# Loading w_down in pairs of whole rows, and accumulating both halves of its columns at once

## The chip, the cores and the metric

The kernel runs on one core of a Trainium2 chip. What is measured is device time in microseconds (us). A core has a tensor engine (PE; its weight loads are shown as PEld), a vector engine (DVE), a scalar engine (ACT), GpSimd (POOL) and the SP engine, which in this kernel issues nearly all the DMA transfers. Transfers run on 16 DMA engines that all queues share. SBUF has 128 partitions; matmuls accumulate in PSUM, in banks of 128 x 512 float32.

## The reference

One decoder block for 256 tokens of width 1024, in float32. A mixer (attention and a convolution), a cross-attention into a memory, and then a mixture of 32 experts, which is the part that matters here:

```python
def expert_step(y, args):
    wg, wu, wd, ge = args
    out = (jax.nn.silu(t @ wg) * (t @ wu)) @ wd
    return y + ge[:, None] * out, None

y, _ = lax.scan(expert_step, jnp.zeros_like(t), (w_gate, w_up, w_down, gates))
```

`w_gate` and `w_up` are [32, 1024, 512] and `w_down` is [32, 512, 1024]: 2 MiB for each matrix of each expert, 192 MiB in all. Each token goes to 2 of the 32 experts; the kernel reads the weights of all 32. The block ends with a residual and an RMS norm.

## The kernel before, in words

**Weights.** Every weight goes through `Ring`: a list of loads in a fixed order (`ring.queue`), 25 slots of SBUF (8 KB in each partition, 1 MiB in all) and `pump`, which issues the next load on SP's queue (line 121) as soon as a slot is free. `ring.take` hands a loaded slot to the code that uses it, and `ring.done` frees it, which issues the next load of the list. So the order of the loads is written out by hand, and SP issues them in that order. In the trace every weight tile is called `w`.

**The experts.** They run in eight groups (`for g in range(NGR)`, line 1140) of four. A group's 24 loads are queued in the order of use: eight of `w_gate` (key `eg`), eight of `w_up` (`eu`), eight of `w_down` (`ed`), 1 MiB each. `w_gate` and `w_up` load in halves of the contraction: partition p gets 4 of its 8 rows, which lie one behind the other in memory (4 x 512 x 4 bytes). `w_down` loads in halves of the columns (`down_cols`): partition p gets 512 of the 1024 columns of 4 rows, so 4 pieces of 2 KB that lie 4 KB apart.

**The products.** The four experts of a group stand side by side on the tensor engine, each in 32 of its 128 columns (32 token places for each expert, `tile_position=(0, 32 * q)`). A float32 matmul shows as two records in the trace. Line 1151 computes `eg` and `eu`, each in one PSUM bank. `hidden_T` takes silu of the one times the other and transposes it to `hT` (lines 985 to 992). Line 1181 computes `ed` = hidden times `w_down`, one column half after the other, each 16 matmuls in a bank of its own; `combine` (lines 1000 and 1002) copies that bank to SBUF on ACT (`yd`) and adds it to the tokens' sums `Y`, which stay in PSUM over all groups. Then `start_group` picks and gathers the tokens of the next group (`tgp`, line 968), transposes the gates (`GSp`, line 975), and the next group begins.

**What sets the order.** A scheduler places each engine's instructions by the order of the code; four PSUM banks are shared by `eg`, `eu`, `hTp`, `ed`, `tgp` and `GSp` in turn, and the tiles `tg` and `yd` share one buffer, so a group's gather waits for the `Y` products of the group before.

**The last group** (g = 7) loads `w_down` in four column slices (512, 256, 128, 128), expert by expert in its matmuls, and the residual and the norm follow slice by slice. Before the last slices it also loads `final_g`, on ACT's queue (line 1163).

Of the kernel before, what the change touches and what calls it, by code (L numbers as in the profile page):

```python
# [18 lines left out]
PSUM = bass.MemoryType.PSUM  # L19

P = 128
# [37 lines left out]
class Ring:  # L59
    """Weight loads in a fixed order through slots of SBUF: a load starts as soon as a slot is free.  # L60
    Larger tensors of the first phase live in slots too, so that their memory joins as they end."""
# [13 lines left out]
    def grow(self, stack, name, n, floats=SLOT):  # L75
        """n more slots, on memory that earlier pools have left"""
        for i in range(n):
            pool = stack.enter_context(self.tc.tile_pool(name="%s_%d" % (name, i), bufs=1, reuse_waits="tile"))
            self.size[pool] = floats
            self.free.append(pool)  # L80
        self.pump(self.first)

    def hold(self, n):
        """keep the next n slots that are freed for spare()"""
        self.held += n

    def spare(self, shape, dt=F32):
        """a slot for another tensor [P, *shape]: the tensor and the slot"""
        pool = self.kept.popleft() if self.kept else self.free.popleft()
        return self.view(pool, shape, dt), pool  # L90
# [7 lines left out]
    def queue(self, key, shape, src, within=None):  # L98
        """within: the load of an earlier key whose slot this one shares, and the columns there"""
        self.todo.append((key, shape, src, within))  # L100

    def pump(self, limit=1000):
        while self.todo and limit:
            key, shape, src, within = self.todo[0]
            if within is None:
                pool = next((p for p in self.free if self.size[p] >= math.prod(shape)), None)
                if pool is None:
                    return
                self.free.remove(pool)
                v = self.view(pool, shape, F32)  # L110
                self.live.append((key, v, pool))
                v = v[:, :, :src.shape[2]]
            else:
                v = next(e[1] for e in self.live if e[0] == within[0])[:, :, within[1]]
            limit -= 1
            self.todo.popleft()
            # the very first in two parts, so that the arithmetic starts sooner
            n = 1 if self.begun else 2
            self.begun = True
            for k in range(0, shape[0], shape[0] // n):  # L120
                self.nc.sync.dma_start(v[:, k:k + shape[0] // n], src[:, k:k + shape[0] // n])
# [18 lines left out]
class Pair:  # L140
    """An operand [P, NJ, S] of 24 significant bits as two of 12; each half of its rows in one slot."""
# [16 lines left out]
def down_cols(g):  # L158
    """column slices of w_down's loads; finer at the end"""
    return [(0, 512), (512, 512)] if g < NE // 4 - 1 else [(0, 512), (512, 256), (768, 128), (896, 128)]  # L160


def body(tc, a, out):
# [55 lines left out]
    # U[s, t] = 1 where s <= t  # L219
# [3 lines left out]
    # the same in bf16, which holds 0 and 1 exactly  # L223
# [4 lines left out]
    # the tensor engine's clock rests when it idles: products nobody reads keep it up meanwhile  # L228
# [16 lines left out]
    # router columns: NG group columns, padding that never wins, NE expert columns  # L245
# [4 lines left out]
    # group of each expert column  # L250
# [18 lines left out]
    # the chunks of v and the forget gate are wider than the others  # L269
# [30 lines left out]
    for g in range(NE // 4):  # L300
        for kind, w in (("eg", w_gate), ("eu", w_up)):
            for h in range(2):
                for q in range(4):
                    wv = w[4 * g + q].rearrange("(p j) f -> p j f", j=NJ)
                    ring.queue((kind, g, h, q), (4, DE), wv[:, 4 * h:4 * h + 4, :])
        for n, (c0, w) in enumerate(down_cols(g)):
            for q in range(4):
                wv = w_down[4 * g + q].rearrange("(p j) n -> p j n", j=4)
                if n < 3:
                    ring.queue(("ed", g, n, q), (4, 256 if n == 2 else w), wv[:, :, c0:c0 + w])  # L310
                else:
                    ring.queue(None, (4, w), wv[:, :, c0:c0 + w], (("ed", g, 2, q), slice(128, 256)))
# [30 lines left out]
    def rsqrt(src, scale, shape, name, pool=None, out=None):  # L343
        """(src * scale + eps) ** -0.5, with one Newton step on the vector engine"""
        pool = pool or small
        r = pool.tile(shape, F32, tag=name + "r", name=name + "r")
        A.activation(r, src, AF.Ln, scale=scale, bias=eps_t)
        A.activation(r, r, AF.Exp, scale=-0.5)
        v = pool.tile(shape, F32, tag=name + "v", name=name + "v")
        V.tensor_scalar(v, src, scale, EPS, op0=OP.mult, op1=OP.add)  # L350
        t = pool.tile(shape, F32, tag=name + "t", name=name + "t")
        if shape[1] == 1:
            V.scalar_tensor_tensor(t, r, r, v, op0=OP.mult, op1=OP.mult)
        else:
            V.tensor_mul(t, r, r)
            V.tensor_mul(t, t, v)
        V.tensor_scalar(t, t, -0.5, 1.5, op0=OP.mult, op1=OP.add)
        out = r if out is None else out
        V.tensor_mul(out, r, t)
        return out  # L360

    def ssq(ss, src, eng):
        """ss [P, 1] = sum of squares along src [P, n]"""
# [8 lines left out]
    def ssq_rstd(src, n, name):  # L372
        """src [P, NT, n] -> rstd [P, NT]"""
# [11 lines left out]
    def split(v):  # L385
        """hi + lo == v exactly, each of 12 significant bits; a few rows of v at a time"""
# [17 lines left out]
    def put_split(pair, j, src, g):  # L404
        """split (src * g) into pair[:, j]"""
# [3 lines left out]
    def transposed(pair, src, g, k0, k1, cols, name):  # L409
        """pair[:, k] = split of g[:, k] * (cols(k) of src)^T, for k in k0 .. k1"""  # L410
# [14 lines left out]
    def normed(src, dst):  # L425
        """rmsnorm, without the gain, of src [P, NT, D] into dst"""
# [11 lines left out]
    def wstat(key, pair, name):  # L438
        """256 columns of a projection, transposed: two [P, S] in PSUM"""
# [10 lines left out]
    def astat(key, pair, n, name, outs=None, first=True, last=True, j0=0, bank=mm_ps):  # L450
        """n columns of a projection, natural: NT tiles [P, n] in PSUM"""
# [85 lines left out]
    # log_sigmoid(f) = min(f, 0) - ln(1 + exp(-|f|)) and its cumulative sum  # L537
# [14 lines left out]
    def cum_2():  # L552
        """-c by head"""
# [6 lines left out]
    def cum_3():  # L560
        """-c the same in every partition: [masked block 0 | block 0 | masked block 1]"""
# [266 lines left out]
    def x_blocks(i, k0, k1):  # L828
        """tT[:, k] = gain * (columns of block k)^T for the tokens of tile i"""
# [24 lines left out]
    # the last products tile by tile, so that the first tile's steps run beside the second's  # L854
# [42 lines left out]
    # experts outside the token's group drop out  # L897
# [15 lines left out]
    # place of each token in its expert's list, from 1  # L913
# [20 lines left out]
    # the experts' sum, [NT][2] tiles [P, 512], grows in PSUM over all groups  # L934
    Yp = [[psY.tile([P, 512], F32, name="Y%d%d" % (i, n)) for n in range(2)] for i in range(NT)]

# [1 line left out]
    last_pick = [None]  # L938

    def pick_mats(key_v, n, eng, SR=None):  # L940
        """S picks tokens into slots; SR has 1/rms for its ones"""
# [11 lines left out]
    def gate_mats(Sv, g_v, n):  # L953
        """the gates in place of S's ones"""
# [7 lines left out]
    def gather(SR, n, tg, j0=0, j1=NJ, step=4):  # L962
        """the normed tokens that SR picks, transposed: tg [P, NJ, n]"""
# [17 lines left out]
    def hidden_T(pg, pu, n, sg=None, hTt=None):  # L981
        """silu(pg) * pu, transposed with f = 4 p + j: [P, 4, n]"""
# [15 lines left out]
    def combine(pd, n, GST, yd, outs, w, first=False, last=False):  # L998
        """add the slots' gated outputs to their tokens in outs, [P, w] for each token tile"""
# [18 lines left out]
    def overflow_table():  # L1018
        """blocks of CAP tokens beyond the first of each expert: their number, experts and thresholds"""
# [29 lines left out]
    def overflow(ntot, eidx, thr):  # L1049
        """the general path: one block of one fuller expert after another"""  # L1050
# [41 lines left out]
    fin = {}  # L1092

    def out_slice(n, c0, w, outs, base, last):
        """Z = outs + base in some columns, and the sum of its squares; all but the last times the gain"""
# [18 lines left out]
    # the group's probability and the two experts' shares of it  # L1114
# [25 lines left out]
    for g in range(NGR):  # L1140
# [29 lines left out]
        for n, (c0, w) in enumerate(down_cols(g)):  # L1170
# [5 lines left out]
            # tile by tile side by side, or as the last weights come in  # L1176
# [16 lines left out]
            else:  # L1193
                for i in range(NT):
                    V.tensor_add(X[:, i, c0:c0 + w], Ycols(c0, w)[i], X[:, i, c0:c0 + w])
                if end:
                    # mean of squares + eps, but for the last columns
# [48 lines left out]
```

## Time and profile before

| what | value |
|---|---|
| device time, 3 runs | 706.91, 707.68, 707.87 us; median 707.68 |
| span of the profiled execution | 705.3 us |
| what lies around the span, to the median | 2.4 us |
| PE busy in the span | 583.4 us (83%) |
| DMA, mean over the span | 337 GB/s, 237.36 MB |
| group 2, from its first `eg` matmul to that of group 3 | 333.26 to 394.79 |
| last group, first `eg` matmul to the end of the span | 642.53 to 705.3 |

The profiled execution's own time is its span, 705.3 us, and the 2.4 us around it that the median of the runs has more. Times below count from the start of the span. A row of the timeline joins neighbouring instructions of one kind: start, length, engine, line, operation, output and inputs, count, and in brackets how long the engine sat idle before it and what ended that. A row of the windows view gives, for one stretch, the busy time and count of each engine, then the granted clock of the tensor engine as a share of full speed, the share of the 16 DMA engines that was busy, and GB/s. The first part of the kernel (mixer, cross-attention, routing) ends at about 250 us; the expert groups fill the rest.

### The profile page before, as it was taken

The page shows a single profiled execution, that of the slowest core. Times are in us where ns is not written, and L with a number is a line of the kernel's source. Part 1 is how long each engine was busy: PE and PEld are TensorE (multiplying, and loading weights), DVE is VectorE, ACT ScalarE, POOL GpSimd, SP SyncE. Part 2 cuts the span into 40 slices and gives each one's busy share as a digit, 9 for nine tenths or more (in the row PEclk, how much of TensorE's full clock was granted, in tenths as well). Part 3 has the DMA queues.
Part 4 walks back from the last instruction along what each step waited for, and adds up shares of the span by engine and source line. Part 5 has one row for each costly group of instructions (what it writes and reads, how often), then busy time and mean ns, then how long its engine had stood idle before and what let it go on. Part 6 is the DMA issues. An engine that isn't in the chain of part 4 may idle for free. (4 is left out here: it accounts for less than half of the span.)

```text
span 705.3 us, 8963 instructions
## 1 busy us (share of the span) xinstructions
PE 583.4 (83%) x3517; PEld 344.8 (49%) x3517; DVE 224.2 (32%) x496; ACT 175.0 (25%) x384; POOL 122.1 (17%) x106
## 2 busy tenths in 40 slices
PE   7999999899899999998657856866796787679685
PEld 4999889678897752525112511511251151125124
DVE  5799789785765620401000100100010010001013
ACT  6474765484444600010000000000000000000023
POOL 5556435493434100000000000000000000000000
PEclk9999999999999999999999999998998999999898
DMA  7979630666756979999999999999999999999993
GB/s 255 358 186 367 235 112 11 228 239 234 302 172 263 339 305 419 409 390 420 418 393 407 419 409 390 421 419 392 408 417 410 390 420 419 392 407 417 413 341 117
DMA packets 91164, 237.36 MB, mean 337 GB/s; under 512 B 11996, under 2 KB 36720, under 8 KB 74736
## 3 DMA queue, kind: packets, MB, share of 16 engines
q1 hardware_dynamic: 90688, 235.72, 87.6%
q10 hardware_dynamic: 432, 1.05, 0.4%
q8 instruction: 28, 0.46, 0.3%
q14 instruction: 16, 0.13, 0.1%
HBM read 235.70 MB, written 1.05 MB: 336 GB/s over the span
## 5 line engine op out<-in xcount | busy, mean ns | idle before, releaser
L1151 PE MATMUL eu<-w,tg 128*32 128x512 f32 x512 | 100.2, 680 | 47.8 <-DMA w<-in_w_up 47.8
L396 POOL TENSOR_TENSOR WL<-w,WH 128x512 fp32r<-128x512 f32 (+1 forms) x80 | 112.2, 1414 | 112.4 <-ACT WH L394 93.0
L1181 PE MATMUL ed<-w,hT 128*32 128x512 f32 (+2 forms) x576 | 90.8, 549 | 29.3 <-DMA w<-in_w_down 23.8
L394 ACT CAST WH<-w 128x512 fp32r<-128x512 f32 (+1 forms) x120 | 72.8, 619 | 47.7 <-PE pmk L401 7.3
L1151 PEld LDWEIGHTS eu<-w,tg 128*32 128x32 f32 x512 | 21.3, 122 | 122.9 <-DMA w<-in_w_up 83.1
L950 POOL TENSOR_SCALAR SR<-S,r 128x128 f32<-128x128 f32 x7 | 4.2, 603 | 397.9 <-PE Y L1002 397.9
L1181 PEld LDWEIGHTS ed<-w,hT 128*32 128x32 f32 x576 | 25.6, 109 | 88.1 <-DMA w<-in_w_down 41.3
L986 DVE TENSOR_TENSOR sgm<-sgm,eu 128x512 f32<-128x512 f32 x8 | 5.5, 688 | 196.4 <-PE eu L1151 167.3
L968 PEld LDWEIGHTS tgp<-SR,X 128*128 128x128 f32 x256 | 61.8, 335 | 11.6 <-ACT SR L949 10.7
L968 PE MATMUL tgp<-SR,X 128*128 128x128 f32 x256 | 63.5, 410 | 4.4 <-ACT SR L949 4.4
L1151 PE MATMUL eg<-w,tg 128*32 128x512 f32 x512 | 63.0, 595 | 3.2 <-DMA w<-in_w_gate 3.2
L492 DVE SCALAR_TENSOR_TENSOR cacc<-z,pT,cacc 128x256 f32<-128x256 f32 x116 | 56.4, 486 | 2.6
L956 DVE TENSOR_TENSOR S<-S,GT 128x256 f32<-128x256 f32 x8 | 3.4, 425 | 133.9 <-POOL SR L950 133.8
L396 DVE TENSOR_TENSOR WL<-w,WH 128x512 fp32r<-128x512 f32 (+1 forms) x40 | 37.5, 938 | 15.6 <-ACT WH L394 15.5
L992 ACT COPY hT<-hTp 128x512 f32<-128x512 f32 x8 | 4.7, 585 | 149.2 <-PE hTp L989 149.2
L1000 ACT COPY yd<-ed 128x512 f32<-128x512 f32 (+2 forms) x18 | 9.7, 538 | 124.0 <-PE ed L1181 124.0
L1002 PE MATMUL Y<-yd,GST 128*128 128x512 f32 (+1 forms) x64 | 30.9, 605 | 8.5 <-ACT yd L1000 8.5
L985 ACT ACTIVATE sgm<-eg 128x512 f32<-128x512 f32 x8 | 4.8, 597 | 131.9 <-PE eg L1151 131.9
L1151 PEld LDWEIGHTS eg<-w,tg 128*32 128x32 f32 x512 | 16.3, 109 | 41.3 <-issue 32.3
L969 DVE TENSOR_TENSOR tg<-tgp,g_norm_ffn_g 128x512 f32<-128x512 f32 (+1 forms) x18 | 11.4, 633 | 53.0 <-PE tgp L968 53.0
L1002 PEld LDWEIGHTS Y<-yd,GST 128*128 128x128 f32 x64 | 10.8, 189 | 28.8 <-ACT yd L1000 21.5
L400 PE MATMUL pmk<-w,WH 128*128 128x256 f32 x64 | 18.8, 294 | 0.0
(332 smaller groups left out, 949.3 us busy)
## 6 DMA issues: line engine op xcount, KB each, us to landing
w<-in_w_up SPq DMA_DIRECT2D x64, 1024.0 KB, 19.9
w<-in_w_gate SPq DMA_DIRECT2D x64, 1024.0 KB, 14.3
w<-in_w_down SPq DMA_DIRECT2D x60, 1024.0 KB, 14.4
w<-in_w_mkv SPq DMA_DIRECT2D x8, 1024.0 KB, 13.3
w<-in_w_in SPq DMA_DIRECT2D x7, 1024.0 KB, 10.4
w<-in_w_out SPq DMA_DIRECT2D x4, 1024.0 KB, 10.8
w<-in_w_mq SPq DMA_DIRECT2D x4, 1024.0 KB, 13.2
w<-in_w_mo SPq DMA_DIRECT2D x4, 1024.0 KB, 6.1
```

What stands on the lines that cost most here:

```text
L394: A.copy(hi, src)
L396: (V if nsplit[0] % 3 == 0 else G).tensor_tensor(lo, src, hi.bitcast(F32), op=OP.subtract)
L400: T.matmul(o, L[0], R[0], start=first, stop=False)
L492: V.scalar_tensor_tensor(dst, z[:, cb, t:t + S], pT[:, 4 * t + cb:4 * t + cb + 1], acc, op0=OP.mult, op1=OP.add)
L968: T.matmul(t[:, j], X[:, i, ja + j::NJ], SR[:, i], start=i == 0, stop=i == NT - 1)
L969: V.tensor_tensor(tg[:, ja:ja + step], t, gff[:, ja:ja + step].unsqueeze(2).to_broadcast([P, step, n]), op=OP.mult)
L985: A.activation(sg, pg[0:n], AF.Silu)
L986: V.tensor_mul(sg, sg, pu[0:n])
L1000: ins = A.copy(yd[:, :w], pd[0:n, :w])
L1002: T.matmul(outs[i], GST[:, i], yd[:, :w], start=first, stop=last)
L1151: T.matmul(o[32 * q:32 * q + 32], tg[:, j, 32 * q:32 * q + 32], ws[q][0][:, jj], start=j == 0, stop=j == NJ - 1, tile_position=(0, 32 * q))
L1181: T.matmul(o[32 * q:32 * q + 32, :w], hh[:, j, 32 * q:32 * q + 32], ws[q][0][:, j, :w], start=j == 0, stop=j == 3, tile_position=(0, 32 * q))
```

## The change

In groups 0 to 6, `w_down` loads in halves of its rows instead of its columns: partition p gets 2 of its 4 rows with all 1024 columns, 8 KB in one piece. There are still eight loads of 1 MiB for each group, through the same slots. The matmuls take the two rows of a load (`jj`) one after the other, and for each row both column halves `n`, in two PSUM banks that are open at once; the first half of the loads is freed after 16 matmuls, the second after the other 16, and both `combine` steps come after all 32. The last group's loads and products stay as they are. The diff also drops comments and docstrings, which are left out here.

```diff
+        if g < NE // 4 - 1:
+
+            for h in range(2):
+                for q in range(4):
+                    wv = w_down[4 * g + q].rearrange("(p j) n -> p j n", j=4)
+                    ring.queue(("ed", g, h, q), (2, D), wv[:, 2 * h:2 * h + 2, :])
+            continue
         for n, (c0, w) in enumerate(down_cols(g)):
             for q in range(4):
                 wv = w_down[4 * g + q].rearrange("(p j) n -> p j n", j=4)
...
         yd = new_yd(P)
-        for n, (c0, w) in enumerate(down_cols(g)):
+        if not last:
+            os_ = [e_ps("ed") for _ in range(2)]
+            for h in range(2):
+                ws = [ring.take(("ed", g, h, q)) for q in range(4)]
+                for jj in range(2):
+                    j = 2 * h + jj
+                    for n in range(2):
+                        for q in range(4):
+                            T.matmul(os_[n][32 * q:32 * q + 32], hh[:, j, 32 * q:32 * q + 32],
+                                     ws[q][0][:, jj, 512 * n:512 * n + 512],
+                                     start=j == 0, stop=j == 3, tile_position=(0, 32 * q))
+                for q in range(4):
+                    ring.done(ws[q][1])
+            for n in range(2):
+                combine(os_[n], P, GST, yd[:, n], Ycols(512 * n, 512), 512, g == 0, False)
+        for n, (c0, w) in enumerate(down_cols(g) if last else []):
             o = e_ps("ed")
```

On SP's queue the loads stay in their places. Around the `w_down` loads of group 0 the queue reads so (128 partitions x 4 pieces of 512 before, x 2048 in one now):

```order
 L121 DMA w<-in_w_gate 128x2048 x7
 L121 DMA w<-in_w_up 128x2048 x7
-L121 DMA w<-in_w_down 128x4x512 x8
+L121 DMA w<-in_w_down 128x2048 x8
 L121 DMA w<-in_w_gate 128x2048 x8
```

Only the shape of the `w_down` loads moved; it is now that of `w_gate` and `w_up`. The same exchange stands in each of the seven groups.

On the tensor engine, group 2 before, from the hidden layer's transpose to the next group's first product (`hTp` the transpose, `ed` the products with `w_down`, `Y_309x` the four sums, `tgp` the gather, `GSp` the gates):

```order
L989 MATMUL hTp<-ident,sgm 128x128 x4
L1181 MATMUL ed<-w,hT 32x512 x17
L1002 MATMUL Y_3090<-yd,GST 128x512
L1002 MATMUL Y_3092<-yd,GST 128x512
L1181 MATMUL ed<-w,hT 32x512 x15
L1002 MATMUL Y_3091<-yd,GST 128x512
L1002 MATMUL Y_3093<-yd,GST 128x512
L968 MATMUL tgp<-SR,X 128x128 x16
L975 MATMUL GSp<-ident,S 128x128 x2
L1151 MATMUL eg<-w,tg 32x512 x32
```

And the same place after the change, where line 1181 has become 1185, 1002 has become 1009 and the others moved by 7:

```order
L996 MATMUL hTp<-ident,sgm 128x128 x4
L1185 MATMUL ed<-w,hT 32x512 x32
L1009 MATMUL Y_3090<-yd,GST 128x512
L1009 MATMUL Y_3092<-yd,GST 128x512
L1009 MATMUL Y_3091<-yd,GST 128x512
L1009 MATMUL Y_3093<-yd,GST 128x512
L975 MATMUL tgp<-SR,X 128x128 x16
L982 MATMUL GSp<-ident,S 128x128 x2
L1158 MATMUL eg<-w,tg 32x512 x32
```

The first pair of `Y` products moved from the middle of the `ed` matmuls to behind all of them; the number of matmuls is the same.

## Rows read from the trace of the kernel before

**Rows 1.** The page's slices: 40 equal parts of the span, 17.6 us each.
```profile
PE   7999999899899999998657856866796787679685
PEclk9999999999999999999999999998998999999898
DMA  7979630666756979999999999999999999999993
```

**Rows 2.** The page's DMA counts and issues: loads, KB of each, us to landing.
```profile
DMA packets 91164, 237.36 MB, mean 337 GB/s; under 512 B 11996, under 2 KB 36720, under 8 KB 74736
w<-in_w_up SPq DMA_DIRECT2D x64, 1024.0 KB, 19.9
w<-in_w_gate SPq DMA_DIRECT2D x64, 1024.0 KB, 14.3
w<-in_w_down SPq DMA_DIRECT2D x60, 1024.0 KB, 14.4
```

**Rows 3.** The windows view: while w_up, w_down, w_gate/w_up and again w_down land.
```profile
402.00:418.00 16.00, 8.96 (x48) 1.83 (x40) 0.00 (x0) 0.60 (x1) 0.00 (x0) 1.00 1.01 419
422.00:441.00 19.00, 12.08 (x56) 3.01 (x48) 0.69 (x1) 1.17 (x2) 0.00 (x0) 1.00 1.05 392
444.00:461.00 17.00, 15.58 (x82) 9.85 (x77) 2.47 (x5) 0.99 (x2) 0.60 (x1) 1.00 1.02 421
606.00:625.00 19.00, 14.43 (x71) 3.94 (x72) 0.69 (x1) 1.17 (x2) 0.00 (x0) 0.91 1.05 388
```

**Rows 4.** The tensor engine's timeline, group 3 and the start of group 4.
```profile
419.79 3.62 PE L1151 MATMUL eu<-w,tg 128*32 128x512 f32 x26 [1.47 <-DMA w<-in_w_up]
...
434.99 1.98 PE L1002 MATMUL Y<-yd,GST 128*128 128x512 f32 x4 [0.53 <-ACT yd L1000]
441.44 3.62 PE L1181 MATMUL ed<-w,hT 128*32 128x512 f32 x26 [1.63 <-DMA w<-in_w_down]
...
456.34 4.49 PE L1151 MATMUL eg<-w,tg 128*32 128x512 f32 x38
461.38 3.19 PE L1151 MATMUL eg<-w,tg 128*32 128x512 f32 x25 [0.56 <-DMA w<-in_w_gate]
...
466.37 1.05 PE L1151 MATMUL eu<-w,tg 128*32 128x512 f32 x2 [1.36 <-DMA w<-in_w_up]
468.87 1.04 PE L1151 MATMUL eu<-w,tg 128*32 128x512 f32 x2 [1.45 <-DMA w<-in_w_up]
```

**Rows 5.** The windows view: PE's work in one whole group, 3.
```profile
394.79:456.34 61.55, 43.88 (x240) 16.88 (x239) 3.16 (x7) 2.75 (x5) 0.60 (x1) 1.00 1.02 408
```

**Rows 6.** The windows view around the start of the groups.
```profile
250.00:260.00 10.00, 10.00 (x64) 6.61 (x67) 1.50 (x4) 0.00 (x0) 0.00 (x0) 1.00 0.59 219
260.00:270.00 10.00, 10.00 (x94) 2.93 (x86) 0.08 (x1) 0.60 (x1) 0.00 (x0) 1.00 1.02 425
```

**Rows 7.** The view of `in_w_down`, stretch 220 to 252: issues, ns, first and last start.
```profile
L121 SPq DMA_DIRECT2D w<-in_w_down x8: 539/540/622, 224.4 to 243.5; - x8
```

**Rows 8.** SP's waits from 250 to 262: us in total, times, longest.
```profile
SPq L121 <- PE eg L1151: 10.5, 1, 10.5
```

**Rows 9.** SP's timeline: load issues of groups 3 and 4.
```profile
402.34 27.20 SPq L121 DMA_DIRECT2D w<-in_w_down  x8
...
443.95 17.79 SPq L121 DMA_DIRECT2D w<-in_w_up  x8
```

**Rows 10.** The tensor engine's timeline: w_down products of groups 0 and 1.
```profile
272.09 4.48 PE L1181 MATMUL ed<-w,hT 128*32 128x512 f32 x34 [0.67 <-ACT hT L992]
...
318.35 3.62 PE L1181 MATMUL ed<-w,hT 128*32 128x512 f32 x26 [0.94 <-DMA w<-in_w_down]
```

**Rows 11.** The tensor engine's timeline: group 7, last w_up load to first w_down products.
```profile
668.81 3.62 PE L1151 MATMUL eu<-w,tg 128*32 128x512 f32 x26 [1.47 <-DMA w<-in_w_up]
673.27 0.75 PE L989 MATMUL hTp<-ident,sgm 128*128 128x128 f32 x4 [0.84 <-DVE sgm L986]
```

**Rows 12.** The chain that ended last, its first piece: start, us, what.
```profile
674.80 8.91 PE ed L1181 x34
```

## What the change will do to the time: the prediction

> **What bounds the kernel now.** I read the page's slices first, then the windows view stretch by stretch, then the tensor engine's timeline with what ended its idle times. In the slices the DMA engines are at 9 tenths from the sixteenth slice on, that is from 15 x 17.6 = 264 us, nearly to the end, while PE mostly stands at 6 to 8 [rows 1]. So the expert groups are fed by a stream of weights. The timeline confirms it: in a steady group PE waits for `w_up`, then for `w_down`, a little for `w_gate`, and again for `w_up` [rows 4], and of the 61.55 us from one group's first `eg` product to the next it is busy 43.88 [rows 5].
>
> The stream is not equally fast everywhere. Where `w_up` or `w_gate` lands it moves 419 and 421 GB/s, where `w_down` lands 392 and 388 [rows 3]. The busy share of the engines does not fall there (1.05 against 1.01 and 1.02): they work as much and move less. The page says what differs: its packets under 8 KB are 74,736 of 91,164 [rows 2], and the 16,428 others are nearly the 128 loads of `w_gate` and `w_up` with 128 packets of 8 KB each (16,384). A `w_down` load of 1 MiB in pieces of 2 KB is 512 packets.
>
> The time of a load comes cleanest from the ends of PE's waits. The last `w_up` load of group 3 lets PE go at 419.79, the last of its eight `w_down` loads at 441.44, the last of the next eight, `w_gate`, at 461.38 [rows 4]. Eight loads with pieces of 2 KB thus took 21.65 us, eight with pieces of 8 KB 19.94.
>
> **The change, part by part.**
>
> *Eight loads with pieces of 8 KB.* A new `w_down` load has just the shape of a `w_gate` load, on both sides: in memory 8 KB in one piece for each partition, 16 KB from one partition to the next; in SBUF one slot. I give it the same time: 21.65 - 19.94 = 1.71 us saved in each group whose `w_down` loads lie in the saturated stream. The windows give less, since their stretches are not cut exactly at the loads: 8.39 MB at 390 GB/s (the mean of the two rows) are 21.51 us, at 420 GB/s 19.97, a saving of 1.54. I take 1.71, as it has all eight loads in it, and keep 1.54 for the range.
>
> The row on packet size can be set against a rule. The Trainium skill (page "DMA: Bandwidth & Descriptors", section "Why small descriptors are slow") puts a fixed overhead of about three cycles on each packet, beside one cycle for 32 bytes: as an estimate 67 cycles for 2 KB and 4 x 64 + 3 = 259 for 8 KB, so 3.4% less time, 0.73 us in a group and 703.3 us for the kernel. The two waits above show 7.9%; by them it is the sum that follows. The rows decide, and the rule's result is among the rivals.
>
> *How many groups.* Seven groups change, but group 0 lies elsewhere. Its loads are issued from 224.4 to 243.5 [rows 7], and its `w_down` products begin at 272.09 after a wait for `hT`, not for a load [rows 10]. Between 250 and 260 the stream stands at 219 GB/s and a busy share of 0.59 [rows 6], because SP waits 10.5 us for slots that PE's first `eg` products free [rows 8]; from 260 on it is saturated at 425 [rows 6]. Landing group 0's `w_down` earlier moves nothing: 0 us. Groups 1 to 6 are in the stream; the last `w_down` load of group 1 already ends a wait of PE [rows 10]. So 6 x 1.71 = 10.3 us.
>
> *The Y products, moved.* Before, the first pair (1.98 us, after 0.53 us for ACT) lay between the two halves of the loads, in time that PE would have waited [rows 4]. Now both pairs come behind the last load. PE's way from there to the next group's first `eg` product was 456.34 - 441.44 = 14.90 us; it grows by 1.98, to 16.9 (the second ACT copy runs beside the first pair, so one such wait stays, as before). The first half of `eg` then ends not at +19.4 but at +21.4, some 1.4 us after the last `w_gate` load at +19.94: the 0.56 us of waiting at 461.38 goes, and the next `w_up` waits, 1.36 and 1.45 us for single loads, take up what is left [rows 4]. The stream itself doesn't wait for PE there. Cost 0. Without that cover it would be 6 x 1.4 = 8.4 us.
>
> *Two banks at once.* The number of matmuls and weight loads stays, four experts still stand side by side, and the banks used in a group are as many. I cost it at nothing: 34 records of line 1181 take 4.48 us [rows 10], and 34 are the 32 of the first half and two of the second, so PE passes from one bank to the other without a stall. A gain is excluded, as nothing is left out. The upper end is each record alone, half of the 1.05 us that two take one after the other [rows 4]; that is the last rival. I take the row of line 1181 itself.
>
> *SP's queue.* Eight `w_down` issues occupy it for 27.20 us, eight `w_up` for 17.79 [rows 9]. The new ones should go as the latter. SP runs ahead of the transfers (19.9 and 14.4 us from issue to landing [rows 2]), so nothing waits for that: 0. It will ask for slots some 5 us earlier; these were freed a whole group before, since 25 slots hold 24 loads of a group and one more.
>
> *The end.* The last group is as before. From its last `w_up` load, which ends a wait at 668.81, PE runs without a wait for a load through `hT` [rows 11] and the `w_down` products that begin the final chain [rows 12]. So 705.3 - 668.81 = 36.5 us behind the last `w_up` load stay, and what the stream gains before it reaches the end whole.
>
> Sum: the profiled execution has a span of 705.3 us; 705.3 - 10.3 = 695.0. With the 2.4 us that the median of the runs has beyond that span, 697.4 us. By the lower saving 6 x 1.54 = 9.2, 698.5.
>
> **The rivals.**
>
> *Part of the difference stays.* If only half of the 1.71 us is due to the packets, and the rest to where `w_down` lies or how it shares the engines, 5.1 us go: 702.6. For it: the trace has no `w_down` load in large pieces. Against: the new loads equal those of `w_gate` in everything that the trace shows. The skill's three cycles, above, would end near here.
>
> *No change.* The loads keep 388 to 392 GB/s because it is the tensor and not the piece that is slow: 707.7. The Trainium skill speaks for this one (same page, "Specifications"): it puts the smallest transfer for line rate at 512 bytes, and 2 KB is well above. By that rule the two rates in the windows should be one; the trace disagrees, with 390 against 420 GB/s.
>
> *Group 0 counts too*, if its loads hold up the `w_gate` loads behind them: 7 x 1.71 = 12.0, 695.7. Against: SP waits for slots there [rows 8].
>
> *Slower: PE becomes the bound.* If a matmul could not run beside its neighbour of another bank, the 64 records of a group's `ed` would take 64 x 0.525 = 33.6 us in place of some 8.1 (4.48 and 3.62 [rows 10]). PE's 43.88 [rows 5] would be 69.4, more than the stream's new 61.55 - 1.71 = 59.8; over six groups 6 x (69.4 - 61.55) = 47 us, about 755. It decides once `ed` costs more than 8.1 + 17.7 = 25.8 us in a group, since PE has 61.55 - 43.88 = 17.7 us free; below that the stream hides it. Against: PE passes from bank to bank now without a stall.
>
> A smaller matter lies in all cases: the granted clock is at its lower level (1.2 of 2.4 GHz) in short stretches, as in group 6, where the mean over 19 us is 0.91 [rows 3]. In front of a load it costs nothing, as PE waits there anyway; in the last 36.5 us it would cost a microsecond or two.
>
> **How the numbers follow.** My forecast gets 0.84, half of the difference 0.06, no change 0.04, group 0 as well 0.03, slower 0.03. The forecast's own range is 696.3 to 698.9: the lower saving, the runs' spread of about 0.5 us to either side, and a microsecond earlier should the deeper queue help. For 8 in 10 I give 695.5 to 700.5, which takes in group 0 and a slow stretch at the end, and leaves out half, no change and slower, 0.13, and a rest. About 0.2%, or 1.4 us, is what a measurement here can tell from no change: faster 0.93 (0.84 + 0.06 + 0.03), the same 0.04, slower 0.03.
>
> **What would show it.** In the new profile the windows where `w_down` lands should read near 420 GB/s in groups 1 to 6, as for `w_gate`, and only the last group's below; packets under 8 KB should fall by 7 x 8 x 512 = 28,672. From the last `w_up` load's wait to the last `w_down` load's should be 19.9 us, from group to group about 59.8, and the way from the last `w_down` load to the next `eg` product 16.9. SP should issue eight `w_down` loads in about 18 us. Group 0's times should stay, as should the 36.5 us at the end. The prediction is wrong if `w_down` stays at 390 GB/s, if PE's waits for loads vanish from the groups (then PE bounds), or if the stream shows gaps that end with a slot.

## The result, and the profile after

| | before | after |
|---|---|---|
| device time, median of 4 runs | 707.71 us (706.91 to 707.87) | 697.25 us (696.63 to 698.14) |
| ratio, with its 95% interval | | 0.9837 [0.9801, 0.9873] |
| span of the profiled execution | 705.3 us | 695.1 us |
| last `w_up` load of the last group ends PE's wait | 668.81 | 658.67 |
| PE busy in the span | 583.4 us | 598.3 us |
| DMA, mean over the span | 337 GB/s | 341 GB/s |

The kernel is faster by 10.5 us; 697.4 was predicted, and a span of 695.0. PE is busy for 15 us longer and the kernel still ends sooner, so the time did not come from PE. One run of the experiment `g0old`, at 1701.43 us, and one of the kernel before, at 986.55 us, lie far outside all others and are left out below. I read the page first, for the packets and the issues, and its slices for the stream.

The page of the kernel after: the slices of 17.4 us (DMA busy share, GB/s), and its count of packets.

```profile
DMA  7979640765747879999999999999999999999993
GB/s 253 358 185 365 229 144 1 241 225 206 304 168 257 339 287 420 421 419 418 420 421 418 420 421 421 418 421 420 422 418 420 419 421 419 419 420 419 405 344 114
DMA packets 69660, 237.36 MB, mean 341 GB/s; under 512 B 11996, under 2 KB 36720, under 8 KB 46064
```

Packets under 8 KB fell from 74,736 [rows 2] to 46,064, by the 28,672 that the changed loads were to lose. From the sixteenth slice on the stream moves 418 to 422 GB/s up to the last group; the DMA engines' busy share reads 9 as before [rows 1]. Now two stretches in which `w_down` lands, the start of the groups and one whole group. The columns are those of [rows 3]: the last three are granted clock, DMA share and GB/s.

```profile
402.00:418.00 16.00, 8.85 (x52) 1.97 (x54) 0.00 (x0) 0.00 (x0) 0.00 (x0) 1.00 1.01 418
594.00:612.00 18.00, 13.32 (x68) 3.51 (x68) 0.69 (x1) 0.59 (x1) 0.00 (x0) 1.00 1.01 419
250.00:260.00 10.00, 10.00 (x64) 6.63 (x67) 1.51 (x4) 0.00 (x0) 0.00 (x0) 1.00 0.55 211
392.44:452.32 59.88, 47.13 (x240) 18.68 (x239) 3.16 (x7) 2.76 (x5) 0.60 (x1) 1.00 1.01 420
```

While `w_down` lands the stream now moves 418 and 419 GB/s at a share of 1.01, where it moved 392 and 388 at 1.05 [rows 3]. The slow start, 211 GB/s at 0.55, is still there [rows 6]. The last row is group 3 from its first `eg` product to the next group's: 59.88 us in place of 61.55, with 47.13 us of PE in it in place of 43.88 [rows 5].

The tensor engine's timeline over group 3 after, from the last `w_up` load to the next group's first `w_up` loads (1158 was 1151, 1185 was 1181, 1009 was 1002).

```profile
416.45 3.62 PE L1158 MATMUL eu<-w,tg 128*32 128x512 f32 x26 [1.45 <-DMA w<-in_w_up]
...
422.35 3.48 PE L1185 MATMUL ed<-w,hT 128*32 128x512 f32 x12 [0.68 <-ACT hT L999]
426.42 4.40 PE L1185 MATMUL ed<-w,hT 128*32 128x512 f32 x24 [0.60 <-DMA w<-in_w_down]
431.41 1.90 PE L1185 MATMUL ed<-w,hT 128*32 128x512 f32 x4 [0.59 <-DMA w<-in_w_down]
...
436.40 3.62 PE L1185 MATMUL ed<-w,hT 128*32 128x512 f32 x20 [0.59 <-DMA w<-in_w_down]
439.95 3.70 PE L1009 MATMUL Y<-yd,GST 128*128 128x512 f32 x8
444.22 7.94 PE L975 MATMUL tgp<-SR,X 128*128 128x128 f32 x32 [0.57 <-ACT SR L956]
...
452.32 7.22 PE L1158 MATMUL eg<-w,tg 128*32 128x512 f32 x63
...
461.33 1.05 PE L1158 MATMUL eu<-w,tg 128*32 128x512 f32 x2 [1.10 <-DMA w<-in_w_up]
463.83 1.05 PE L1158 MATMUL eu<-w,tg 128*32 128x512 f32 x2 [1.45 <-DMA w<-in_w_up]
```

Three readings. From the last `w_up` load to the last `w_down` load: 436.40 - 416.45 = 19.95 us, where [rows 4] had 21.65. From there to the next `eg` product: 452.32 - 436.40 = 15.92 us, where it was 14.90. And the wait of `eg` for `w_gate` (0.56 us at 461.38 [rows 4]) is gone; the next `w_up` loads end waits of 1.10 and 1.45 us, so PE has caught up with the stream.

SP's timeline after: eight issues of `w_down`.

```profile
399.02 17.77 SPq L121 DMA_DIRECT2D w<-in_w_down  x8
```

The eight `w_down` issues stand in a stretch of 17.77 us in place of 27.20 [rows 9]; those of `w_gate` and `w_up` behind them in 17.79 us each. Such a stretch also holds what SP waits between two issues. On the page, the time from issue to landing is now this, the same for `w_gate` and `w_up`:

```profile
w<-in_w_down SPq DMA_DIRECT2D x60, 1024.0 KB, 19.9
```

The tensor engine's timeline after, groups 0 and 1, and then the last group from its last `w_up` load: the `ed` products of its four column slices.

```profile
272.11 7.07 PE L1185 MATMUL ed<-w,hT 128*32 128x512 f32 x64 [0.68 <-ACT hT L999]
...
316.44 3.62 PE L1185 MATMUL ed<-w,hT 128*32 128x512 f32 x20 [0.59 <-DMA w<-in_w_down]
...
658.67 3.62 PE L1158 MATMUL eu<-w,tg 128*32 128x512 f32 x26 [1.49 <-DMA w<-in_w_up]
...
664.65 8.83 PE L1203 MATMUL ed<-w,hT 128*32 128x512 f32 x36 [0.78 <-ACTq L1060]
...
676.13 3.75 PE L1203 MATMUL ed<-w,hT 128*32 128x256 f32 x36
...
681.36 1.99 PE L1203 MATMUL ed<-w,hT 128*32 128x128 f32 x24
...
684.36 2.46 PE L1203 MATMUL ed<-w,hT 128*32 128x128 f32 x32
```

Group 0 begins its `ed` products at 272.11, as at 272.09 before [rows 10]; group 1's last `w_down` load comes 318.35 - 316.44 = 1.91 us earlier; the last `w_up` load of the last group 668.81 - 658.67 = 10.14 us earlier [rows 11]. Behind that the end takes 695.1 - 658.67 = 36.4 us, as before (36.5). The gain grows group by group: the last `w_up` loads of groups 2 to 7 let PE go 1.62, 3.34, 5.62, 7.12, 8.49 and 10.14 us earlier than before, in steps of 1.37 to 2.28 us. It is made in the stream, in the six groups named, and nowhere else.

### The profile page after: what moved, and what is told of

It reads as the page before. It is cut to its first block, busy times and chain, and to the rows that moved or that the text cites. A ratio compares the mean times of both kernels' runs of the same rounds, so it can differ in the third digit from the quotient of the medians.

```text
span 695.1 us, 8957 instructions
## 1 busy us (share of the span) xinstructions
PE 598.3 (86%) x3517; PEld 353.8 (51%) x3517; DVE 224.1 (32%) x496; ACT 175.1 (25%) x384; POOL 122.2 (18%) x106
## 2 busy tenths in 40 slices
DMA packets 69660, 237.36 MB, mean 341 GB/s; under 512 B 11996, under 2 KB 36720, under 8 KB 46064
## 3 DMA queue, kind: packets, MB, share of 16 engines
q10 hardware_dynamic: 432, 1.05, 0.4%
HBM read 235.70 MB, written 1.05 MB: 341 GB/s over the span
## 5 line engine op out<-in xcount | busy, mean ns | idle before, releaser
L1158 PE MATMUL eu<-w,tg 128*32 128x512 f32 x512 | 102.7, 715 | 45.0 <-DMA w<-in_w_up 45.0
L1185 PE MATMUL ed<-w,hT 128*32 128x512 f32 x448 | 89.1, 598 | 16.9 <-DMA w<-in_w_down 12.2
L975 PEld LDWEIGHTS tgp<-SR,X 128*128 128x128 f32 x256 | 62.0, 336 | 10.8 <-ACT SR L956 10.0
L1185 PEld LDWEIGHTS ed<-w,hT 128*32 128x32 f32 x448 | 22.0, 109 | 79.0 <-issue 39.3
L1158 PE MATMUL eg<-w,tg 128*32 128x512 f32 x512 | 61.0, 594 | 0.0
L1158 PEld LDWEIGHTS eg<-w,tg 128*32 128x32 f32 x512 | 18.4, 109 | 34.0 <-issue 27.4
L1009 PE MATMUL Y<-yd,GST 128*128 128x512 f32 (+1 forms) x64 | 29.0, 593 | 1.1 <-ACT yd L1007 1.1
L1009 PEld LDWEIGHTS Y<-yd,GST 128*128 128x128 f32 x64 | 11.4, 189 | 18.8 <-issue 10.5
## 6 DMA issues: line engine op xcount, KB each, us to landing
w<-in_w_up SPq DMA_DIRECT2D x64, 1024.0 KB, 19.9
w<-in_w_gate SPq DMA_DIRECT2D x64, 1024.0 KB, 19.9
w<-in_w_down SPq DMA_DIRECT2D x60, 1024.0 KB, 19.9
```

The source lines that it names most:

```text
L975: T.matmul(t[:, j], X[:, i, ja + j::NJ], SR[:, i], start=i == 0, stop=i == NT - 1)
L1009: T.matmul(outs[i], GST[:, i], yd[:, :w], start=first, stop=last)
L1158: T.matmul(o[32 * q:32 * q + 32], tg[:, j, 32 * q:32 * q + 32], ws[q][0][:, jj], start=j == 0, stop=j == NJ - 1, tile_position=(0, 32 * q))
L1185: T.matmul(os_[n][32 * q:32 * q + 32], hh[:, j, 32 * q:32 * q + 32], ws[q][0][:, jj, 512 * n:512 * n + 512], start=j == 0, stop=j == 3, ti ...
```

## The experiments

Each kernel below is the one after with one edit, timed in five rounds against the kernel before on the same chip. The theory: each packet of a load has a fixed price on the DMA engines, and 8 KB pieces have a quarter of the packets of 2 KB pieces. The rivals: that the gain came with the new order of the products or of the rows; that it belongs to the tensor `w_down` and not to the pieces; that the gaps in memory cost and not the packets; that group 0 or SP's queue had a part in it. SP's queue has no run of its own; the traces have to settle it.

**Pieces of 2 KB again, all else as after** (`two2k`).

```diff
+            if key is not None and key[0] == "ed" and shape == (2, D):
+                for c in (0, 512):
+                    self.nc.sync.dma_start(v[:, :, c:c + 512], src[:, :, c:c + 512])
+                continue
```

> The changed kernel, but each w_down load of groups 0 to 6 is issued as two transfers, one for each column half, so that the pieces are 2 KB again; slots, bytes, row pairs and the order of all products stay as in the changed kernel. Theory (the time of a load is set by its packets): eight megabytes in 2 KB pieces take 21.65 us again, 1.71 us a group in six groups come back: 697.25 + 10.3 = 707.5 us. Rival (the order of the products and the Y pairs moved to the end made the gain): 697 us, as the order is kept. Rival (the number of transfers counts, not of packets): more than 707.5, since there are twice as many.

Measured: 707.68 us (706.82 to 712.06), ratio 0.9986 [0.9961, 1.001]: the whole gain is gone, with the new order of the products kept. The tensor engine's timeline of this kernel, two last `w_up` loads, the last two waits for `w_down` and a last `w_gate` load:

```profile
359.94 3.62 PE L1162 MATMUL eu<-w,tg 128*32 128x512 f32 x26 [1.47 <-DMA w<-in_w_up]
...
421.49 3.62 PE L1162 MATMUL eu<-w,tg 128*32 128x512 f32 x26 [1.45 <-DMA w<-in_w_up]
...
440.48 1.05 PE L1189 MATMUL ed<-w,hT 128*32 128x512 f32 x2 [0.31 <-DMA w<-in_w_down]
441.81 3.62 PE L1189 MATMUL ed<-w,hT 128*32 128x512 f32 x20 [0.29 <-DMA w<-in_w_down]
...
463.09 3.19 PE L1162 MATMUL eg<-w,tg 128*32 128x512 f32 x25 [0.87 <-DMA w<-in_w_gate]
```

The group's length, 421.49 - 359.94 = 61.55 us, is that of before. One thing differs: PE's last wait for `w_down` ends after 20.32 us and the last `w_gate` load comes 21.28 us behind it; the sum, 41.60, is that of before (461.38 - 419.79 = 41.59 [rows 4]). That wait is for the fifteenth of the sixteen half loads: a half takes 21.65 / 16 = 1.35 us, the last two waits end 1.33 us apart, and 15 x 1.35 = 20.3. The sixteenth was issued at 432.3 and such transfers land 10.8 us after their issue, so at about 443.1, while PE works; from there the eight `w_gate` loads take 20.0 us, as pieces of 8 KB do.

**Pieces of 4 KB** (`row4k`): a load has rows h and h + 2 in place of two neighbours.

```diff
-                    ring.queue(("ed", g, h, q), (2, D), wv[:, 2 * h:2 * h + 2, :])
+                    ring.queue(("ed", g, h, q), (2, D), wv[:, h::2, :])
...
-                    j = 2 * h + jj
+                    j = h + 2 * jj
```

> The changed kernel, but a w_down load of groups 0 to 6 takes rows h and h+2 of each four in place of two neighbours, so one transfer of 1 MiB has pieces of 4 KB that lie 8 KB apart. Theory (each packet costs a fixed bit: 21.65 - 19.94 = 1.71 us for eight times 384 packets more): 256 packets in place of 128 add 8 x 128 / (8 x 384) of it, 0.57 us a group, 3.4 us in six: 700.7 us. Rival (what counts is that the bytes of a partition lie in one piece, in memory rows): as slow as 2 KB pieces, 707.5 us. Rival (4 KB is already long enough, as everything from 512 bytes on): 697.3 us.

Measured: 702.24 us (699.73 to 705.97), ratio 0.9913 [0.9881, 0.9945], its profiled execution with a span of 698.0. The median is 1.5 us above what was expected, and the six runs scatter over 6 us, so the size is read from the trace. The timeline, last `w_up` and last `w_down` load of group 3:

```profile
415.87 3.62 PE L1158 MATMUL eu<-w,tg 128*32 128x512 f32 x26 [1.47 <-DMA w<-in_w_up]
...
436.33 3.62 PE L1185 MATMUL ed<-w,hT 128*32 128x512 f32 x20 [0.64 <-DMA w<-in_w_down]
```

And the windows view of it while `w_down` lands:

```profile
418.00:434.00 16.00, 12.50 (x55) 3.17 (x48) 0.69 (x1) 0.59 (x1) 0.00 (x0) 1.00 1.03 410
```

Eight loads take 20.46 us, 0.51 more than in pieces of 8 KB, with 8 x 128 = 1,024 more packets. Pieces of 2 KB take 1.70 more with 3,072 more packets. Groups 2 to 6 agree: 19.95 to 20.02 us with 8 KB, 20.44 to 20.63 with 4 KB, 21.57 to 21.66 with 2 KB in the kernel before. Rate (420, 410, 390 GB/s) and busy share (1.01, 1.03, 1.05) stand in steps in the same way. The price goes with the number of packets.

**`w_gate` in pieces of 2 KB** (`gate2k`): the same cost put on another tensor, in groups 1 to 7; `w_down` stays as after.

```diff
-                    ring.queue((kind, g, h, q), (4, DE), wv[:, 4 * h:4 * h + 4, :])
+                    apart = g > 0 and kind == "eg"
+                    ring.queue((kind, g, h, q), (4, DE), wv[:, h::2, :] if apart else wv[:, 4 * h:4 * h + 4, :])
```

The products of `eg` take their rows to match.

> The changed kernel, but w_gate of groups 1 to 7 loads every other row in place of four neighbours: 1 MiB still, in 2 KB pieces 4 KB apart. Theory (packets, whatever the tensor): the eight w_gate loads of a group take 21.65 us in place of 19.94, seven groups lie in the stream: 697.25 + 7 x 1.71 = 709.2 us. Rival (w_down was slow for where it lies, or for its four rows per partition): 697.3 us.

Measured: 709.32 us (707.7 to 712.1), ratio 1.0003 [0.9979, 1.0026]. The timeline, last `w_up`, `w_down` and `w_gate` loads:

```profile
422.25 3.62 PE L1159 MATMUL eu<-w,tg 128*32 128x512 f32 x26 [1.45 <-DMA w<-in_w_up]
...
442.22 3.62 PE L1186 MATMUL ed<-w,hT 128*32 128x512 f32 x20 [0.61 <-DMA w<-in_w_down]
...
463.99 3.19 PE L1159 MATMUL eg<-w,tg 128*32 128x512 f32 x25 [1.40 <-DMA w<-in_w_gate]
```

`w_down` 19.97 us, `w_gate` 21.77: the two have changed places. It is the piece and not the tensor.

**Packets of 2 KB from unbroken rows** (`perm2k`): each load as two transfers of one row, 4 KB in one piece in memory, written to two places of SBUF.

```diff
+            if key is not None and key[0] == "ed" and shape == (2, D):
+                v = v.rearrange("p j n -> p (j n)").rearrange("p (n j c) -> p j n c", n=2, j=2)
+                for j in range(2):
+                    self.nc.sync.dma_start(v[:, j], src[:, j].rearrange("p (n c) -> p n c", c=512))
+                continue
...
-                                     ws[q][0][:, jj, 512 * n:512 * n + 512],
+                                     ws[q][0][:, n, 512 * jj:512 * jj + 512],
```

> In groups 0 to 6 each w_down load is issued as two transfers of one whole row each: 4 KB in one piece in memory for each partition, but written to two places of 2 KB that lie 4 KB apart in SBUF (the matmuls read the new places). So the number of pieces is that of the kernel before, while the memory side is read in pieces of 4 KB, as in the kernel with pieces of 4 KB. If the price is one for each packet, wherever its bytes lie: about 92,000 packets on the page, a group of about 61.6 us from one last w_up wait to the next, and 707.5 us (706.5 to 709), as the kernel before. Rival, that the gaps in memory cost and not the packets: a group of 60.4 us or less and 702.2 us or less, as with pieces of 4 KB. A third, that only the number of transfers counts (two for each load): 707.5 as well, but the kernel with two transfers of half the columns speaks against it only together with the packets; the landing of a 512 KB transfer would tell, 1.35 us there.

Measured: 709.98 us (706.66 to 713.07), ratio 1.0026 [1.0006, 1.0047]. The median lies 1 us above the range that I gave and 1.5 above the kernel before. In the profiled execution, whose span is 711.2, the excess stands already ahead of the expert groups: the first `eg` product starts at 255.82 in place of 251.60, at a granted clock of 0.97 over that stretch in place of 0.99. I did not settle why; the groups tell the theories apart. The window of its trace while `w_down` lands, and then two last `w_up` loads of its timeline:

```profile
424.00:440.00 16.00, 13.51 (x69) 3.76 (x70) 0.69 (x1) 0.59 (x1) 0.00 (x0) 0.90 1.05 387
```

```profile
362.52 5.22 PE L1163 MATMUL eu<-w,tg 128*32 128x512 f32 x26 [1.50 <-DMA w<-in_w_up]
...
424.05 5.17 PE L1163 MATMUL eu<-w,tg 128*32 128x512 f32 x26 [1.47 <-DMA w<-in_w_up]
```

A group takes 61.53 us and the stream moves 387 GB/s, as with 2 KB pieces in memory, and not the 60.4 us (415.87 - 355.51 in `row4k`) and 410 GB/s of 4 KB pieces. The gaps in memory cost nothing here; the packets do: its page counts 92,061, as that of `two2k`, where the kernel before has 91,164, with nearly all of the difference under 512 B. Nor is it the split in SBUF, since the four pieces of a load of before lie one behind the other in their slot and take as long. The number of transfers has no part in it either: the loads of before were one transfer each and took as long.

**One column half after the other, with loads of 8 KB pieces** (`halves`). The lines that these replace are not shown.

```diff
+            ws = [[ring.take(("ed", g, h, q)) for q in range(4)] for h in range(2)]
+            for n in range(2):
+                o = e_ps("ed")
+                for j in range(4):
+                    for q in range(4):
+                        T.matmul(o[32 * q:32 * q + 32], hh[:, j, 32 * q:32 * q + 32],
+                                 ws[j // 2][q][0][:, j % 2, 512 * n:512 * n + 512],
+                                 start=j == 0, stop=j == 3, tile_position=(0, 32 * q))
+                combine(o, P, GST, yd[:, n], Ycols(512 * n, 512), 512, g == 0, False)
...
```

> The changed kernel's loads, but the products of groups 0 to 6 in the order of before, one column half after the other, each in its own bank, with all eight loads taken first and freed after all 32 matmuls. Theory (the loads alone give the gain, the two open banks only let PE keep pace): PE starts most of the 32 matmuls some 10 us later and is 3 to 4 us later at the next group, which the waits for w_up take up; 697.3 us, at most 1 more. Rival (two banks at once are part of the gain): between 699 and 707 us.

Measured: 697.1 us (696.36 to 698.08), ratio 0.9831 [0.9805, 0.9857]. The timeline from its last `w_down` load of group 3:

```profile
437.65 2.76 PE L1183 MATMUL ed<-w,hT 128*32 128x512 f32 x14 [0.60 <-DMA w<-in_w_down]
440.34 1.99 PE L1009 MATMUL Y<-yd,GST 128*128 128x512 f32 x4
442.26 1.06 PE L1183 MATMUL ed<-w,hT 128*32 128x512 f32 x6
444.06 1.98 PE L1009 MATMUL Y<-yd,GST 128*128 128x512 f32 x4 [0.75 <-ACT yd L1007]
...
454.67 7.07 PE L1158 MATMUL eg<-w,tg 128*32 128x512 f32 x64
```

With the order written in halves the scheduler still mixes the two: 58 of the 64 `ed` records (12, 24, 4, 4 and 14) stand ahead of the first pair of `Y`, so 26 of the second half's 32 ran before the first half was combined. `halves` is therefore no test of one bank at a time; it shows what a later copy costs. A wait of 0.75 us for ACT's copy shows before the second pair of `Y`, and the way from the last load to the next `eg` product is 17.0 us in place of 15.92. The time is the same: 1.1 us more on PE's way in each group is hidden by the stream.

**Group 0 as before** (`g0old`).

```diff
-        if g < NE // 4 - 1:
+        if 0 < g < NE // 4 - 1:
...
-        if not last:
+        if 0 < g and not last:
...
-        for n, (c0, w) in enumerate(down_cols(g) if last else []):
+        for n, (c0, w) in enumerate(down_cols(g) if last or g == 0 else []):
```

> The changed kernel, but group 0 loads and multiplies w_down as before (2 KB pieces, one column half after the other); groups 1 to 6 keep the change. Theory (group 0's loads land some 20 us before their use, at a time when the stream stops for slots): 697.3 us, as the changed kernel. Rival (group 0 counts too): 1.7 us more, 699.0 us.

Measured: 696.8 us (696.64 to 698.14), ratio 0.9836 [0.9802, 0.9869], span 695.0. The timeline of its groups 0 and 1:

```profile
272.02 4.48 PE L1203 MATMUL ed<-w,hT 128*32 128x512 f32 x34 [0.68 <-ACT hT L999]
...
316.62 3.62 PE L1185 MATMUL ed<-w,hT 128*32 128x512 f32 x20 [0.58 <-DMA w<-in_w_down]
```

Group 0 waits for `hT` either way, and group 1's last `w_down` load comes at 316.62 or 316.44: the loads of group 0 are worth nothing.

**Experts one after the other** (`serial`): in groups 0 to 6 the four products of one expert and load follow each other, so that hardly anything stands side by side.

```diff
-                for jj in range(2):
-                    j = 2 * h + jj
-                    for n in range(2):
-                        for q in range(4):
+                for q in range(4):
+                    for n in range(2):
+                        for jj in range(2):
+                            j = 2 * h + jj
```

> The changed kernel, but in groups 0 to 6 the matmuls of one load go one after the other (expert by expert), so that no two experts stand side by side: in the last group, which has this order, 16 matmuls take 8.83 us in place of 4.5. Theory (the stream bounds, PE has room): 32 matmuls take up to 17.7 us in place of 8.1 where the loads are all there, as in group 0 and 1, and hide between the landings elsewhere, since one load's share is 2.2 us and a load lands every 2.49; 697.3 us, at most 1 more. Rival (PE's time in the groups counts): 6 x 9.6 = 58 us more, 755 us.

Measured: 697.97 us (696.24 to 701.09), ratio 0.9852 [0.9817, 0.9887]. The timeline of its group 3 and the start of group 4:

```profile
426.73 15.85 PE L1185 MATMUL ed<-w,hT 128*32 128x512 f32 x64 [0.67 <-ACT hT L999]
...
454.83 7.07 PE L1158 MATMUL eg<-w,tg 128*32 128x512 f32 x64
...
465.35 1.04 PE L1158 MATMUL eu<-w,tg 128*32 128x512 f32 x2 [1.45 <-DMA w<-in_w_up]
```

The 64 records take 15.85 us where they take 7.07 side by side (group 0 after), and PE is back at waiting for `w_up` in the next group. So PE's room in a group is real, and the price of a record that stands alone is 15.85 / 64 = 0.25 us, not the 0.525 of my last rival.

**The last group's experts in pairs** (`tail`): nothing of the theory, but the next thing on the path once the stream ends earlier.

```diff
-                order = [(j, q) for q in range(4) for j in range(4)]
+                order = [(j, q) for q0 in (0, 2) for j in range(4) for q in (q0, q0 + 1)]
```

> The changed kernel, but in the last group the matmuls of w_down go in two pairs of experts side by side (experts 0 and 1, then 2 and 3) in place of expert by expert. Theory (behind the last w_up load PE bounds, with its serial order; 8.83, 3.75, 1.99 and 2.46 us for the four column slices, while the loads of these slices have landed): the first slice ends when its last load is there plus 2.2 us, about 1.9 us earlier, the later ones come up to the loads, whose last lands at 682.4, and the end follows it by some 9 us in place of 12.7: about 693.5 us. Rival (the last group's loads bound the end): 697 us.

Measured: 693.99 us (693.3 to 697.64), ratio 0.9793 [0.9759, 0.9827]. On the same chip and in the same round of runs `g0old` took 696.8 (696.64 to 698.14), so it beats both kernels, by some 3 us against the one after. Its profiled execution was the slowest of the six; the timeline of its end:

```profile
662.81 5.30 PE L1158 MATMUL eu<-w,tg 128*32 128x512 f32 x26 [1.49 <-DMA w<-in_w_up]
...
670.47 6.89 PE L1203 MATMUL ed<-w,hT 128*32 128x512 f32 x38 [0.77 <-ACTq L1060]
...
680.00 2.42 PE L1203 MATMUL ed<-w,hT 128*32 128x256 f32 x40
...
683.92 1.07 PE L1203 MATMUL ed<-w,hT 128*32 128x128 f32 x18
...
686.00 1.58 PE L1203 MATMUL ed<-w,hT 128*32 128x128 f32 x32
```

The first slice's products take 6.89 us in place of 8.83; the three others 2.42, 1.07 and 1.58 in place of 3.75, 1.99 and 2.46: 5.1 us in all. In this execution the `eu` products ahead of them took 5.30 us in place of 3.62 (from there to the end the mean granted clock was 0.86, after it was 0.95), which leaves 3.4; from the last `w_up` load to the end of the span it is 33.1 us in place of 36.4, so 3.3.

## Why the prediction was right, step by step

**What bounds the kernel** was read rightly: a stream of loads that PE waits for in every group. `gate2k` and `two2k` make the stream slower and the kernel slower by as much; `serial` and `halves` make PE slower and the time stays.

**Eight loads, 1.71 us.** Measured: 21.65 - 19.95 = 1.70. Shown by the four kernels with pieces of 2 and 4 KB: it is a price for each packet, the same on `w_down` and `w_gate`, with or without gaps in memory. The rival in which part of the difference stays and the one of no change fall.

The Trainium skill's two statements on it (page "DMA: Bandwidth & Descriptors") do not hold in size. By its section "Specifications" 2 KB should run at line rate; the windows show 388 to 392 GB/s against 418 to 421. By about three cycles for each packet (section "Why small descriptors are slow") I estimated 0.73 us in a group; the runs show 1.70, some 2.3 times as much. The direction, that fewer packets are cheaper, the runs bear out.

**Six groups, not seven.** Right: 10.14 us at the last `w_up` load of the last group against 6 x 1.70 = 10.2, in six steps, and `g0old` is as fast without group 0.

**The moved Y products.** Hidden, as predicted, but mis-sized: the way from the last `w_down` load to the next `eg` product grew by 1.02 us (14.90 to 15.92) and not by 1.98. The step that failed is that one wait for ACT would stay, as before. The kernel before, the second pair of group 3 in PE's timeline:

```profile
445.73 1.98 PE L1002 MATMUL Y<-yd,GST 128*128 128x512 f32 x4 [0.68 <-ACT yd L1000]
```

With that wait it was 4.29 us from the last `w_down` load to the first `Y` product behind it; now it is 3.55. With two open banks ACT copies the first, from 439.25 on, while PE still works on the second, and eight `Y` records run in 3.70 us without a wait, less than twice 1.98. In `halves`, where a wait of 0.75 us for the copy stays, the way is 17.0, near my 16.9.

**Two banks at once, at no cost.** Right for the products themselves: 64 records in 7.07 us in group 0, where before 34 took 4.48 and the other 26 to 30 some 3.62 [rows 10] (side by side). What I did not foresee is that PE's busy time in a steady group rises by 3.25 us, to 47.13 (that of the `ed` records alone by 3.67, from 11.63 to 15.30). While loads still arrive, a load lets four records go that stand alone (1.90 us) where before it was two, as in this row of its group 3:

```profile
427.93 1.04 PE L1181 MATMUL ed<-w,hT 128*32 128x512 f32 x2 [1.19 <-DMA w<-in_w_down]
```

It lies in time in which PE would have waited. The slower rival's 755 us was also too high for its own case, in two terms. It put a group's `ed` before at 8.1 us, where group 3 has 11.63. And it took its price from two records behind a wait (0.525 us each), while in `serial`, the worst order tried, a record costs 0.25 us and the kernel took 697.97. By these two rows PE would have 43.88 - 11.63 + 15.85 = 48.1 us of work in a group, below the stream's 59.88. Why records in short runs behind a wait show twice that price is not settled.

**SP's queue.** The stretch came out as predicted, 17.77 us for eight issues, and all three kinds of load now take 19.9 us from issue to landing. That the issues occupy SP for so long was a misreading. The view of `in_w_down` in group 3, before and after, with the shortest, median and longest issue in ns:

```profile
L121 SPq DMA_DIRECT2D w<-in_w_down x8: 551/2508/9272, 402.3 to 427.0; - x8
L121 SPq DMA_DIRECT2D w<-in_w_down x8: 327/327/328, 399.0 to 416.5; - x8
```

After, eight issues take 2.6 us of the 17.77; between them SP waits, nearly always for an earlier load to land (256 us from 330 to 640). Before, single issues took up to 9.3 us. The stream was not held up by that: each of these loads was issued 14.4 us or more ahead of its landing, and the DMA engines' share was 1.05 [rows 3].

**The end.** Right: 36.4 us against 36.5, and the stream's gain reached it whole. It is PE there and not the loads: `tail` shortens it by 3.3 us with the loads left alone. How much more could be had there before the last loads bind was not tried.

The forecast of 697.4 us lies 0.15 us from the median. That hit does not test the two terms that were mis-sized, the `Y` products and the two banks: both lie in time in which PE waits for loads.

## What to carry to other kernels

Where a stream of loads bounds a kernel, compare its rate tensor by tensor in windows and read the packet count beside them: two rates at one busy share of the DMA engines, with different piece sizes, mean time that can be gained, and the ends of the consumer's waits give the size of it. Cut such a load along the dimension that leaves whole rows, even if the consumer must then hold two sums open; what that costs the consumer is hidden as long as it still waits for loads. And count the groups in which the stream really runs: a load that waits for a slot, or is waited for by nobody, gains nothing.

## What the runs showed of the hardware that I had not expected

- The price of a packet is nearly a constant: 1,024 more of them cost 0.51 us and 3,072 more 1.70 us on 16 engines, so 0.51 x 16 / 1,024 = 8.0 ns and 1.70 x 16 / 3,072 = 8.9 ns of one engine's time. It is the same when the memory side is unbroken and only the place in SBUF is split (61.53 us for a group against 61.55).
- An issue on SP takes longer for a load with more packets: for group 0 0.54 us with 512 packets [rows 7] and 0.33 with 128, and in the saturated stream of group 3 0.55 to 9.27 us with 512 and 0.33 with 128. What holds the long ones up is not shown.
- Four experts side by side ran these 64 float32 records 15.85 / 7.07 = 2.2 times as fast as one after the other (`serial`), not 4 times.
